# adaLN weights and folded Fourier rows loaded through GpSimd's queue, folds in buffers of their own, three maps in slots

## The chip, the cores and the metric

One core of a Trainium2 chip runs the whole program. The metric is the device time of one execution in microseconds (us); the kernel before takes 1999.18 us, the median of 3 executions (1997.12 to 1999.19). The engines are TensorE (PE), VectorE (DVE), ScalarE (ACT), GpSimd (POOL) and SyncE (SP). A DMA is issued by an instruction on one of these engines, and waits in that engine's instruction order; the profile writes SPq and POOLq for the issuing queue of SP and of POOL.

## The reference, cut to what matters

```python
D_MODEL, SEQ, CTX_LEN, D_FF, N_MOD, DEPTH = 1024, 512, 256, 2816, 9, 2
def modulate(x, shift, scale): return rmsnorm(x) * (1 + scale) + shift
def swiglu(h, w_gu, w_down):
    g, u = jnp.split(h @ w_gu, 2, axis=-1)
    return (jax.nn.silu(g) * u) @ w_down
def fourier_mixer(h, w_out, b_out):
    hg = h.astype(jnp.float32).reshape(Bn, L, C_GROUPS, C_GROUP_CH)
    f = jnp.fft.fftn(hg, axes=(1, 3), norm='ortho').real
    return f.reshape(Bn, L, D_MODEL).astype(h.dtype) @ w_out + b_out
for l in range(DEPTH):                   # layer 0: attention || gMLP, layer 1: Fourier
    m = jnp.split((jax.nn.silu(c) @ ada_w[l] + ada_b[l])[:, None, :], N_MOD, axis=-1)
    x = x + 0.5 * m[2] * swiglu(modulate(x, m[0], m[1]), ffn_w_gu[l, 0], ffn_w_down[l, 0])
    ...                                  # the context tokens the same, in layer 0, with c_ctx
    h = modulate(x, m[3], m[4])
    x = x + m[5] * y                     # y: attention and gMLP, or the Fourier mixer, of h
    x = x + 0.5 * m[8] * swiglu(modulate(x, m[6], m[7]), ffn_w_gu[l, 1], ffn_w_down[l, 1])
return rmsnorm(x, final_norm_g)
```

Everything is float32. The nine modulation vectors `m` of a layer (adaLN: shift, scale and gate of three sub-layers) are a matrix product of one row with a 1024 x 9216 matrix.

## The kernel before, in words

The latent stream stays in SBUF as eight tiles `xs[k]` of 128 channels x 512 tokens. Each product is made of three matmuls (`mm3`, L167 to L171): a weight is split by ACT into a high part `wh` (L162) and by DVE into the rest `wl` (L164), and so is each activation. All weights come through SP's queue: `raw` and `rk` tiles (L161), loaded in the order in which they are used.

**adaLN.** The modulation is not made on PE. The class `Ada` loads 128 rows of the transposed adaLN matrix at a time into a tile `aw` of 128 x 1024 floats (512 KB, `load`, L235), and DVE multiplies it with SiLU(c) on all partitions and sums along the row (`dot`, L240, output `junk`), which gives one column of `modx` (for the context, of `modc`). There are 160 such loads. Those of layer 0 are spread over the first feed-forward network and the attention, with three `aw` buffers; those of layer 1 lie in the last feed-forward network of layer 0 and the first of layer 1, with two buffers (`apool1`, bufs=2).

**A feed-forward network** (`ffn`) goes over 22 slices j of 128 inner channels in chunks of 6, 6, 6 and 4. For each slice PE makes g and u (24 matmuls each), ACT the SiLU, DVE `prod` (L358) = SiLU * u, ACT its high part `ah` (L359), DVE its rest `al` (L360). After a chunk PE multiplies the `ah`, `al` of the chunk with the down weights into `dps`, and DVE adds that to x (L272). A step's extra work is handed to it by hooks: `extra2(j)` puts modulations and folds into step j of the first network of layer 1.

**The folds.** The Fourier mixer's last product uses weights `wf` folded beforehand: `fold(m)` loads 128 rows of wf (`fr`, L1115), DVE adds and subtracts halves (`fold`, L1118 to L1120), ACT and DVE split the result (L1126, L1127), and two stores of 512 KB each put it into `wfd` in DRAM (L1129). Fold 8 holds only a few rows and begins with a memset (L1124). Folds 0 to 8 are made at steps j = 8 to 16 of that network. The `fr` tile is one of the two `aw` buffers of `apool1`.

**The maps.** In the Fourier stage `folded(m)` loads the two parts of map m (`wh` and `wl`, 512 KB each, L1196) from `wfd` into `wpool` tiles, three buffers of each; products `fe` and `fo` use them. `spool` holds equal slots of 128 x 512 floats (`slot`) for activations.

The order of each engine's instructions is set by a scheduler from priorities; `with behind(mark(...))` holds what is in it to the place at which the code calls it.

Of the kernel before, what the change touches and what calls it, by code (L numbers as in the profile page):

```python
# [11 lines left out]
F32 = mybir.dt.float32  # L12
F32R = mybir.dt.float32r
# [6 lines left out]
P = 128  # L20
D = 1024
# [15 lines left out]
DOWN_AT = (0, 0, 0, 0, 0)  # L37

FOLD_AT = 8
IDLE = (5, 8)  # L40
ADA0 = dict(early=4, late=4, first_down=2, down=1, ctx=1)
ADA1 = dict(begin=2, end=20, a=2.2, b=3)
# [6 lines left out]
def kernel(ctx, tc, a):  # L49
    nc = tc.nc  # L50
# [8 lines left out]
    def slot(shape, dtype, name):  # L59
        return spool.tile(shape, dtype, tag="s", name=name)  # L60
# [34 lines left out]
    def nm(s):  # L95
        uid[0] += 1
        return f"{s}_{uid[0]}"

    DVE, ACT, SP = mybir.EngineType.DVE, mybir.EngineType.Activation, mybir.EngineType.SP

    def mark(*engines):

        traced = nc.cur_bb.bb.instructions
        return [next(i for i in reversed(traced) if i.engine == e) for e in engines or (DVE, ACT)]

    @contextmanager
    def behind(last):

        with ExitStack() as st:
            for i in last or ():  # L110
                st.enter_context(tc.issue_after(i))
            yield
# [9 lines left out]
    def banks(name):  # L122

        return pairs.tile([P, 2, 512], F32, tag="pp", name=nm(name))
# [94 lines left out]
    class Ada:  # L219
# [12 lines left out]

        def load(self, l, i):
            w = self.pool.tile([P, D], F32, tag="aw", name=nm("aw"))
            nc.sync.dma_start(w, a["adaT"][l, i])  # L235
            return w

        def dot(self, w, out, c):
# [17 lines left out]
    def col(m, j, k):  # L256
        return m[:, 8 * j + k:8 * j + k + 1]
# [85 lines left out]
    def first_w(l, i):  # L343

        return [kept(a["wgu"][2 * l + i, j, q]) for j in range(2) for q in range(2)]
# [207 lines left out]
    apool = st0.enter_context(tc.tile_pool(name="apool", bufs=3))  # L553
# [98 lines left out]
    def some(us):  # L652
        budget[0] += us
        while jobs and budget[0] >= jobs[0][0]:
            c, f = jobs.pop(0)
            budget[0] -= c
            with behind(mark(DVE, ACT, SP) if len(jobs) < len(rest) or not rest else None):
                f()
# [21 lines left out]
    def mix_w(n):  # L680
        while len(ws) < n:
            ws.append(kept(srcs[len(ws)]))

    mid, _ = ffn(0, 0, h, lambda m: col(modx[0], 2, m), tails, [(0, 8), (8, 5), (13, 5), (18, 4)],
              ctx={"h": hc1, "gate": lambda m: col(modc, 2, m)}, extra=extra0, start=(start_w, start), ahead=lambda: None,
              between=lambda: mix_w(4))
# [63 lines left out]
    def weights(src):  # L750
        w = load_w(src, [P, KD, P])
        return lambda k: (w[0][:, k], w[1][:, k])
# [73 lines left out]
    for t in range(4):  # L826
        for g in range(4):
            i = 4 * t + g
# [24 lines left out]
    for hd in range(1, 4):  # L853
        w = weights(a["wk"][hd])
# [217 lines left out]
    apool = st3.enter_context(tc.tile_pool(name="apool1", bufs=2))  # L1072
# [35 lines left out]
    wfd = [dram.tile([P, 2, D], F32, name=f"wfd{m}") for m in range(KD + 1)]  # L1108

    def fold(m):  # L1110
        raw = apool.tile([P, D], F32, tag="aw", name=nm("fr"))
        sm = raw
        if m < KD:
            sm = apool.tile([P, D], F32, tag="fold", name=nm("fold"), bufs=1)
            nc.sync.dma_start(raw, a["wf"][m].rearrange("p k c -> p (k c)"))  # L1115
            lower, upper = (raw.rearrange("p (k c) -> p k c", k=KD)[:, i::2] for i in range(2))
            both = [sm[:, b:b + 512].rearrange("p (k c) -> p k c", k=4) for b in (0, 512)]
            nc.vector.tensor_tensor(both[0], lower, upper, ALU.add)  # L1118
            nc.vector.tensor_tensor(both[1], upper, lower, ALU.subtract)
            nc.vector.memset(sm[0:1, 512:1024], 0.0)  # L1120
            hi = raw
        else:
            hi = apool.tile([P, D], F32, tag="fold", name=nm("fold"), bufs=1)
            nc.vector.memset(raw, 0.0)  # L1124
            nc.sync.dma_start(raw[0:4].rearrange("g (m c) -> g m c", m=KD), a["wf"][:, 0, 1::2, :].rearrange("m g c -> g m c"))
        nc.scalar.copy(hi.bitcast(F32R), sm)  # L1126
        nc.vector.tensor_tensor(sm.bitcast(F32R), sm, hi, ALU.subtract)  # L1127
        for i, t in enumerate((hi, sm)):
            nc.sync.dma_start(wfd[m][:, i], t)  # L1129

    def extra2(j, m=None):
        if m is None and j < ADA1["end"]:
            some(ADA1["b"])
        if m is None and FOLD_AT <= j <= FOLD_AT + KD:
            fold(j - FOLD_AT)

    mid, w1 = ffn(0, 1, h3, lambda m: col(modx[0], 8, m), tails, chunks, mid=mid, w1=w1,
                  ahead=lambda: first_w(1, 0), extra=extra1)
# [55 lines left out]
    def stored(m, wh, wl):  # L1194
        for i, t in enumerate((wh, wl)):
            nc.sync.dma_start(t.bitcast(F32), wfd[m][:, i])  # L1196

    def folded(m):
        wh = wpool.tile([P, 1024], F32R, tag="wh", name=nm("wh"))
        wl = wpool.tile([P, 1024], F32R, tag="wl", name=nm("wl"))  # L1200
        stored(m, wh, wl)
        return [(wh[:, i * P:i * P + P], wl[:, i * P:i * P + P]) for i in range(8)]
# [8 lines left out]
    for t0, g in [(t0, g) for t0 in (0, 2) for g in range(4)]:  # L1211
        if 2 * t0 + g in (4, 5):
            ps = banks("G")[:, :, :256]
        else:
            ps = bank("G").rearrange("p (t c) -> p t c", t=2)
        for t in range(2):
            ts_ = slice((t0 + t) * P, (t0 + t) * P + P)
            for kt in range(2):
                hk = h5[2 * g + kt]
                cs = slice(256 * kt, 256 * kt + 256)  # L1220
                nc.tensor.matmul(ps[:, t], hk[0][:, ts_], tc_[0][:, cs], start=kt == 0, stop=False)
                nc.tensor.matmul(ps[:, t], hk[0][:, ts_], tc_[1][:, cs], start=False, stop=False)
                nc.tensor.matmul(ps[:, t], hk[1][:, ts_], tc_[0][:, cs], start=False, stop=kt == 1)
        pair = [slot([P, 2, 256], F32R, nm("gt")) for _ in range(2)]
        for t in range(2):
            rt = rtok[:, t0 + t, 0:1]
            nc.scalar.activation(pair[0][:, t], ps[:, t], AF.Copy, scale=rt)
            nc.vector.scalar_tensor_tensor(pair[1][:, t], ps[:, t], rt, pair[0][:, t].bitcast(F32),
                                           ALU.mult, ALU.subtract)
            gh[t0 + t][g] = (pair[0][:, t], pair[1][:, t])  # L1230
        for q in range(2):
            nc.vector.tensor_tensor(nyd[:, t0:t0 + 2, q, g], pair[q][:, :, 128].bitcast(F32), pair[q][:, :, 0].bitcast(F32), ALU.subtract)
        if t0 == 0 and g == 0:
            constant()
            mid[0]()
            mid[1]()
    COS, SIN = slice(0, 258), slice(256, 512)
    ef, of = [], []
    for g in range(4):
# [40 lines left out]
    for m in range(KD):  # L1280
        w = folded(m)
# [22 lines left out]
        if m == 2:  # L1304
            w1 = first_w(1, 1)
    idle(IDLE[0])
    rstd6(SEG[0])
    idle(IDLE[1])
    end6(SEG[0])
# [135 lines left out]
```

## Time and profile before

| what | value |
| --- | --- |
| time, median of 3 (lowest, highest) | 1999.18 us (1997.12, 1999.19) |
| profiled execution's own time | 2007.54 us |
| span of the profiled execution | 2005.8 us |
| mean granted TensorE clock | 0.996 of full speed |
| PE busy | 1968.6 us, 98% |
| DVE busy | 1194.8 us, 60% |
| ACT busy | 706.0 us, 35% |
| POOL busy | 22.3 us, 1% |
| moved by SP's DMA queue (q1) | 288.37 MB, 44.5% of 16 engines' span |
| moved by POOL's DMA queue (q0) | 4.20 MB, 0.8% |

The profile shows one execution, which took 8.4 us longer than the median of the timed ones, and 1.74 us of it lie outside its span. PE is busy nearly throughout, so the places to look at are the few in which it isn't, or in which its matmuls are slow.

### The profile page before, as it was taken

Reading aid. Unit: us, or ns where it says so; the run is one execution under the profiler, and the core shown is the slowest. Engines: PE = TensorE matmul, PEld = TensorE weight load, DVE = VectorE, ACT = ScalarE, POOL = GpSimd, SP = SyncE. Lnnn points to the kernel's source line nnn. Section 1 sums busy time; section 2 is a strip of 40 time slices with the busy share of each in tenths; the row PEclk is TensorE's granted clock in tenths of the full one; section 3 lists DMA queues with packets and bytes.
Section 4 is the critical chain, followed back from the end, with each engine's and each line's share of the span. In section 5 each row is a group of like instructions: output and inputs, shape, how many; then the busy total and the mean of one; then the engine's idle time right before and its main releaser. Section 6 shows DMA issues by size and latency. Waiting matters only on the chain.

```text
span 2005.8 us, 27095 instructions
## 1 busy us (share of the span) xinstructions
PE 1968.6 (98%) x10687; PEld 1704.3 (85%) x10687; DVE 1194.8 (60%) x2160; ACT 706.0 (35%) x1161; POOL 22.3 (1%) x49
## 2 busy tenths in 40 slices
PE   7999999999999999999999999999999999999998
PEld 5878899888998877988888898887878998888887
DVE  7984567466386569845555565566673673334344
ACT  4332224212264257632222343232333642222324
POOL 0000000000000110000000000000000000000000
PEclk9999999999999999999999999999999999999999
DMA  8773346456213632244545533568673142323331
GB/s 293 255 240 116 103 150 223 155 182 215 84 43 111 170 109 64 75 149 135 186 140 178 171 113 107 170 210 274 221 267 121 61 147 83 110 82 108 105 100 43
DMA packets 96742, 294.31 MB, mean 147 GB/s; under 512 B 11717, under 2 KB 15077, under 8 KB 96614
## 3 DMA queue, kind: packets, MB, share of 16 engines
q1 hardware_dynamic: 94950, 288.37, 44.5%
q0 software_dynamic: 1664, 4.20, 0.8%
q8 instruction: 84, 1.38, 0.3%
q14 instruction: 44, 0.36, 0.1%
HBM read 270.50 MB, written 11.53 MB: 141 GB/s over the span
## 4 chain that ended last, share of the span: by engine, by line
PE 85%; DVE 6%; DMA 5%; ACT 2%; issue 1%; SPq 0%; DVEq 0%; ACTq 0%
PE dps L171 9%; PE dps L169 9%; PE dps L170 9%; PE g L169 6%; PE g L170 6%; PE g L171 6%; PE u L169 6%; PE u L170 6%; PE u L171 6%; DMA aw<-in_adaT 3%; PE gc L171 2%; PE gc L170 2%; PE gc L169 2%; DVE junk L240 2%; PE gu L169 1%; PE pj L169 1%
## 5 line engine op out<-in xcount | busy, mean ns | idle before, releaser
L162 ACT CAST wh<-raw 128x1024 fp32r<-128x1024 f32 (+3 forms) x309 | 299.1, 969 | 593.8 <-PE dps L171 257.3
L164 DVE TENSOR_TENSOR wl<-raw,wh 128x1024 fp32r<-128x1024 f32 (+3 forms) x309 | 346.8, 1124 | 258.5 <-ACT wh L162 255.9
L169 PE MATMUL u<-hh,wh 128*128 128x512 f32 (+1 forms) x656 | 249.3, 380 | 0.0
L170 PE MATMUL g<-hh,wl 128*128 128x512 f32 (+1 forms) x656 | 248.9, 379 | 0.0
L169 PE MATMUL g<-hh,wh 128*128 128x512 f32 (+1 forms) x656 | 248.9, 379 | 0.0
L171 PE MATMUL u<-hl,wh 128*128 128x512 f32 (+1 forms) x656 | 248.7, 379 | 0.0
L171 PE MATMUL g<-hl,wh 128*128 128x512 f32 (+1 forms) x656 | 248.7, 379 | 0.0
L170 PE MATMUL u<-hh,wl 128*128 128x512 f32 (+1 forms) x656 | 248.7, 379 | 0.0
L169 PE MATMUL dps<-ah,wh 128*128 128x512 f32 x576 | 226.9, 394 | 6.3 <-ACT ah L359 6.3
L171 PE MATMUL dps<-al,wh 128*128 128x512 f32 x576 | 226.3, 393 | 1.2 <-DVE al L360 1.2
L170 PE MATMUL dps<-ah,wl 128*128 128x512 f32 x576 | 226.3, 393 | 0.0
L272 DVE SCALAR_TENSOR_TENSOR x<-dps,modx,x 128x512 f32<-128x512 f32 (+1 forms) x176 | 106.6, 624 | 142.0 <-PE dps L171 141.6
L240 DVE SCALAR_TENSOR_TENSOR junk<-aw,cb 128x1024 bf16<-128x1024 f32 x144 | 175.4, 1218 | 21.3 <-DMA aw<-in_adaT 21.3
L358 DVE TENSOR_TENSOR prod<-sil,u 128x512 f32<-128x512 f32 (+1 forms) x82 | 54.0, 658 | 180.6 <-PE u L171 178.3
L171 PEld LDWEIGHTS g<-hl,wh 128*128 128x128 f32 x656 | 123.5, 188 | 23.1
L171 PEld LDWEIGHTS u<-hl,wh 128*128 128x128 f32 x656 | 123.5, 188 | 23.0
L169 PEld LDWEIGHTS u<-hh,wh 128*128 128x128 f32 x656 | 123.5, 188 | 23.1
L170 PEld LDWEIGHTS u<-hh,wl 128*128 128x128 f32 x656 | 123.4, 188 | 23.1
L169 PEld LDWEIGHTS g<-hh,wh 128*128 128x128 f32 x656 | 123.5, 188 | 22.8
L170 PEld LDWEIGHTS g<-hh,wl 128*128 128x128 f32 x656 | 123.6, 188 | 22.6
L356 ACT ACTIVATE sil<-g 128x512 f32<-128x512 f32 (+1 forms) x82 | 47.3, 577 | 265.9 <-PE g L171 265.9
L169 PEld LDWEIGHTS dps<-ah,wh 128*128 128x128 f32 x576 | 109.3, 190 | 29.7 <-ACT ah L359 7.5
(355 smaller groups left out, 3693.7 us busy)
## 6 DMA issues: line engine op xcount, KB each, us to landing
raw<-in_wgu SPq DMA_DIRECT2D x172, 512.0 KB, 3.6
aw<-in_adaT SPq DMA_DIRECT2D x160, 512.0 KB, 4.5
raw<-in_wdn SPq DMA_DIRECT2D x72, 384.0 KB, 3.1
raw<-in_wdn SPq DMA_DIRECT2D x16, 512.0 KB, 3.6
rk<-in_wdn SPq DMA_DIRECT2D x32, 256.0 KB, 3.8
rk<-in_wgu SPq DMA_DIRECT2D x24, 256.0 KB, 3.7
raw<-in_wdn SPq DMA_DIRECT2D x16, 320.0 KB, 2.9
wfd<-fr SPq DMA_DIRECT2D x9, 512.0 KB, 2.9
```

The lines of the kernel that those rows point to most:

```text
L162: nc.scalar.copy(wh, raw)
L164: nc.vector.tensor_tensor(wl, raw, wh.bitcast(F32), ALU.subtract)
L169: nc.tensor.matmul(ps, w[0], x[0], start=first, stop=False)
L170: nc.tensor.matmul(ps, w[1], x[0], start=False, stop=False)
L171: nc.tensor.matmul(ps, w[0], x[1], start=False, stop=last)
L240: nc.vector.scalar_tensor_tensor(junk, w, 1.0, c, ALU.mult, ALU.mult, accum_out=out)
L272: nc.vector.scalar_tensor_tensor(xt, ps, gt, xt, ALU.mult, ALU.add)
L356: nc.scalar.activation(s, g, AF.Silu)
L358: nc.vector.tensor_tensor(p, s, u, ALU.mult)
```

## The change: what it does

The loads of `aw`, the loads of `fr` in folds 0 to 7 and all stores to `wfd` are issued by POOL instead of SP (the few rows of fold 8 are still loaded by SP). `fr` gets a buffer of its own instead of one of the two `aw` buffers. `fold` is held to the place at which it is called. Maps 0, 1 and 2 are loaded in quarters of 256 KB (tile `we`, 12 loads by SP) into slots of `spool` and no longer into `wpool` tiles, so that the three buffers there begin with map 3. Line numbers of the changed kernel are larger by 2, after the fold's code by 3 and more.

```diff
+EARLY = (0, 1, 2)
...
         def load(self, l, i):
             w = self.pool.tile([P, D], F32, tag="aw", name=nm("aw"))
-            nc.sync.dma_start(w, a["adaT"][l, i])
+            nc.gpsimd.dma_start(w, a["adaT"][l, i])
             return w
...
     def fold(m):
-        raw = apool.tile([P, D], F32, tag="aw", name=nm("fr"))
+        raw = apool.tile([P, D], F32, tag="fr", name=nm("fr"), bufs=1)
         sm = raw
         if m < KD:
             sm = apool.tile([P, D], F32, tag="fold", name=nm("fold"), bufs=1)
-            nc.sync.dma_start(raw, a["wf"][m].rearrange("p k c -> p (k c)"))
+            nc.gpsimd.dma_start(raw, a["wf"][m].rearrange("p k c -> p (k c)"))
...
         for i, t in enumerate((hi, sm)):
-            nc.sync.dma_start(wfd[m][:, i], t)
+            nc.gpsimd.dma_start(wfd[m][:, i], t)
 
     def extra2(j, m=None):
...
         if m is None and FOLD_AT <= j <= FOLD_AT + KD:
-            fold(j - FOLD_AT)
+            with behind(mark(DVE, ACT, SP)):
+                fold(j - FOLD_AT)
...
+    early = {}
+
+    def folded_early(m):
+
+        w = [[slot([P, 512], F32R, nm("we")) for _ in range(2)] for _ in range(2)]
+        for i in range(2):
+            for b in range(2):
+                nc.sync.dma_start(w[i][b].bitcast(F32), wfd[m][:, i, 512 * b:512 * b + 512])
+        early[m] = [tuple(w[i][q // 4][:, q % 4 * P:q % 4 * P + P] for i in range(2)) for q in range(8)]
+
     def folded(m):
+        if m in early:
+            return early[m]
...
+    for m in EARLY:
+        folded_early(m)
     COS, SIN = slice(0, 258), slice(256, 512)
```

**The start of the program.** SP's rows in the kernel before, from the last two of the eight loads of x on: `vecs` holds biases, `raw` the first weights.

```order
L557 DMA x_100<-in_xT 128x512
L557 DMA x_101<-in_xT 128x512
L558 DMA vecs<-in_vecs 128x161
L235 DMA aw_188<-in_adaT 128x1024
L235 DMA aw_192<-in_adaT 128x1024
L161 DMA raw_203<-in_w 128x1024
L235 DMA aw_231<-in_adaT 128x1024
L235 DMA aw_235<-in_adaT 128x1024
L161 DMA raw_246<-in_w 128x1024
```

In the changed kernel POOL begins as follows (the rows named masks.py make an identity matrix):

```order
masks.py:197 MEMSET ident 128x128
L237 DMA aw_188<-in_adaT 128x1024
masks.py:199 ISA
masks.py:199 AFFINE_SELECT ident<-ident 128x128
L237 DMA aw_192<-in_adaT 128x1024
L237 DMA aw_231<-in_adaT 128x1024
L237 DMA aw_235<-in_adaT 128x1024
```

Before, the first two `aw` stood behind all of x and `vecs`, and two more behind the first `raw`. Now they stand at the head of another queue, and behind `vecs` SP goes on with one `raw` after the other.

**The folds, on the issuing queue.** SP's rows in the kernel before around fold 1's stores (`wfd_8140`) and the load of fold 2 (`fr_12339`):

```order
L235 DMA aw_12324<-in_adaT 128x1024 [waits DMAHW4_49,DMAHW0_49,DVE_49]
L161 DMA raw_12524<-in_wdn 128x768 [waits DVE_49]
L1129 DMA wfd_8140<-fr_12244 128x1024 [waits Activation_49]
L1129 DMA wfd_8140<-fold_12245 128x1024 [waits DMAHW3_49,DVE_49]
L235 DMA aw_12329<-in_adaT 128x1024 [waits DMAHW0_49,DVE_49]
L235 DMA aw_12334<-in_adaT 128x1024 [waits DMAHW5_49,DMAHW2_49]
L161 DMA raw_12550<-in_wdn 128x768 [waits DMAHW6_49,DVE_49]
L1115 DMA fr_12339<-in_wf 128x1024 [waits DMAHW7_49,DMAHW4_49,DVE_49]
```

POOL's rows in the changed kernel around the same stores:

```order
L237 DMA aw_12324<-in_adaT 128x1024 [waits DMASW6_49,DVE_49]
L1117 DMA fr_12244<-in_wf 128x1024 [waits DMASW0_49]
L237 DMA aw_12329<-in_adaT 128x1024 [waits DMASW7_49,DVE_49]
L1131 DMA wfd_8140<-fr_12244 128x1024 [waits Activation_49]
L1131 DMA wfd_8140<-fold_12245 128x1024 [waits DVE_49]
L237 DMA aw_12334<-in_adaT 128x1024 [waits DMASW2_49,DVE_49]
L1117 DMA fr_12339<-in_wf 128x1024 [waits DMASW5_49]
```

`aw_12329` moved ahead of the stores of fold 1; `aw_12334` and the load of fold 2 stand behind them, and the latter waits for the landing of a store (DMASW5).

**The same place on DVE.** The kernel before, from fold 1's last subtraction on:

```order
L1127 TENSOR_TENSOR fold_12245<-fold_12245,fr_12244 128x1024
L240 SCALAR_TENSOR_TENSOR junk_12326,modx_89<-aw_12324,cb_8484 128x1024
L252 SCALAR_TENSOR_TENSOR modx_89<-modx_89,vecs 128x1
L164 TENSOR_TENSOR wl_12470<-raw_12472,wh_12471 128x768
L240 SCALAR_TENSOR_TENSOR junk_12331,modx_89<-aw_12329,cb_8484 128x1024
L358 TENSOR_TENSOR prod_12415<-sil_12413,u_12362 128x512
L252 SCALAR_TENSOR_TENSOR modx_89<-modx_89,vecs 128x1
L240 SCALAR_TENSOR_TENSOR junk_12336,modx_89<-aw_12334,cb_8484 128x1024
L360 TENSOR_TENSOR al_12412<-prod_12415,ah_12411 128x512
```

The changed kernel, from the dot with `aw_12329` on:

```order
L242 SCALAR_TENSOR_TENSOR junk_12331,modx_89<-aw_12329,cb_8484 128x1024
L166 TENSOR_TENSOR wl_12470<-raw_12472,wh_12471 128x768
L254 SCALAR_TENSOR_TENSOR modx_89<-modx_89,vecs 128x1
L242 SCALAR_TENSOR_TENSOR junk_12336,modx_89<-aw_12334,cb_8484 128x1024
L360 TENSOR_TENSOR prod_12415<-sil_12413,u_12362 128x512
L254 SCALAR_TENSOR_TENSOR modx_89<-modx_89,vecs 128x1
L1120 TENSOR_TENSOR fold_12340<-fr_12339 128x512
L1121 TENSOR_TENSOR fold_12340<-fr_12339 128x512
L362 TENSOR_TENSOR al_12412<-prod_12415,ah_12411 128x512
```

The dot with `aw_12329` no longer stands right ahead of `prod_12415`; that with `aw_12334` does, and fold 2's two additions stand between `prod_12415` and `al_12412`.

## Rows read from the trace of the kernel before

**Rows 1.** Waits, all engines: total us, times, longest.

```profile
DVE junk L240 <- DMA aw<-in_adaT: 26.0, 20, 4.8
```

**Rows 2.** A window: length, PE, PEld, DVE, ACT, POOL busy (count), clock, DMA share, GB/s.

```profile
50.00:100.00 50.00, 50.00 (x221) 41.10 (x220) 48.60 (x104) 19.88 (x26) 0.00 (x0) 1.00 0.79 256
```

**Rows 3.** The chain that ended last, single pieces: start, length, what.

```profile
4.40 6.02 DMA x<-in_xT
...
19.21 2.08 PE gu L169 x4
...
110.38 5.33 DMA aw<-in_adaT
...
1606.33 7.03 DMA wl<-wfd
```

**Rows 4.** Timeline of DVE near 116 us: start, length, instruction, [wait].

```profile
115.73 1.23 DVE L240 SCALAR_TENSOR_TENSOR junk<-aw,ccb 128x1024 bf16<-128x1024 f32 x1 [1.49 <-DMA aw<-in_adaT]
```

**Rows 5.** Timeline of PE at the same place.

```profile
118.27 0.50 PE L169 MATMUL dps<-ah,wh 128*128 128x512 f32 x1 [1.62 <-ACT ah L359]
...
119.44 0.50 PE L171 MATMUL dps<-al,wh 128*128 128x512 f32 x1 [0.43 <-DVE al L360]
```

**Rows 6.** Timeline of PE at fold 2.

```profile
1367.65 0.39 PE L171 MATMUL dps<-al,wh 128*128 128x512 f32 x1
1370.81 0.79 PE L169 MATMUL dps<-ah,wh 128*128 128x512 f32 x1 [2.77 <-ACT ah L359]
...
1377.13 0.40 PE L171 MATMUL dps<-al,wh 128*128 128x512 f32 x1
```

**Rows 7.** Timeline of DVE there.

```profile
1368.27 1.22 DVE L240 SCALAR_TENSOR_TENSOR junk<-aw,cb 128x1024 bf16<-128x1024 f32 x1 [4.76 <-DMA aw<-in_adaT]
...
1369.42 0.68 DVE L358 TENSOR_TENSOR prod<-sil,u 128x512 f32<-128x512 f32 x1
...
1371.23 0.68 DVE L360 TENSOR_TENSOR al<-prod,ah 128x512 fp32r<-128x512 f32 x1
```

**Rows 8.** Timeline of SP's queue there.

```profile
1359.94 0.42 SPq L1129 DMA_DIRECT2D wfd<-fr  x1
...
1362.44 2.48 SPq L235 DMA_DIRECT2D aw<-in_adaT  x2
```

**Rows 9.** Timeline of PE at fold 7.

```profile
1471.69 0.39 PE L171 MATMUL dps<-al,wh 128*128 128x512 f32 x1
1473.95 0.50 PE L169 MATMUL dps<-ah,wh 128*128 128x512 f32 x1 [1.87 <-ACT ah L359]
...
1479.48 0.39 PE L169 MATMUL dps<-ah,wh 128*128 128x512 f32 x1
```

**Rows 10.** Timeline of DVE there.

```profile
1470.36 0.69 DVE L1118 TENSOR_TENSOR fold<-fr 128x512 f32<-128x512 f32 x1 [1.02 <-DMA fr<-in_wf]
...
1472.23 0.62 DVE L358 TENSOR_TENSOR prod<-sil,u 128x512 f32<-128x512 f32 x1
```

**Rows 11.** Windows of the start and of four stalls, columns as in rows 2.

```profile
2.00:4.00 2.00, 0.63 (x1) 0.49 (x2) 0.00 (x0) 1.22 (x3) 0.00 (x0) 1.00 0.73 251
...
10.00:12.00 2.00, 2.00 (x2) 0.43 (x2) 1.64 (x6) 1.96 (x4) 0.00 (x0) 1.00 1.02 416
...
115.00:120.00 5.00, 2.95 (x12) 1.82 (x11) 4.26 (x8) 2.38 (x4) 0.00 (x0) 1.00 0.87 301
...
1370.00:1375.00 5.00, 4.19 (x9) 2.95 (x10) 4.55 (x10) 1.45 (x2) 0.00 (x0) 0.51 0.72 207
...
1475.00:1480.00 5.00, 4.50 (x13) 3.57 (x14) 4.58 (x7) 2.40 (x3) 0.00 (x0) 0.66 0.94 298
...
1605.00:1610.00 5.00, 4.46 (x37) 4.28 (x36) 4.19 (x10) 0.73 (x2) 0.00 (x0) 1.00 0.93 330
```

**Rows 12.** The page's DMA issues: count, KB each, median us to landing.

```profile
wfd<-fr SPq DMA_DIRECT2D x9, 512.0 KB, 2.9
```

**Rows 13.** Timeline of POOL's queue, one load of 64 rows.

```profile
746.74 0.52 POOL L871 DMA_DIRECT2D k<-roth  x1
```

## The prediction

> **What bounds the kernel now.** The table of busy times comes first: PE is busy for 98% of the span, so the kernel is bound by PE, and only its few gaps and slow stretches can be won. The second view, the waits, tells which of DVE's waits the moved loads have a part in: DVE waits 20 times for an `aw`, 26.0 us in all [rows 1]. That is no loss by itself, as DVE is idle for 40% of the span. It matters where `prod` or `al`, which PE needs, stand behind such a dot. So the third view is PE's timeline, read for gaps, and beside each the timeline of DVE. At full pace PE starts a matmul each 50.00/221 = 0.226 us [rows 2]. There are four places on which the change bears.
>
> *The start.* The first weight product starts at 19.21; what went before is the landing of the last x, 4.40 + 6.02 = 10.42, and the norm made from it [rows 3].
>
> *116 us.* DVE, busy for 48.60 of the 50 us before [rows 2], waits 1.49 for an `aw` [rows 4] that was issued at 110.38 [rows 3]; `prod` stands right behind that dot, and PE waits 1.62 for `ah` and 0.43 for `al` [rows 5]. With two matmuls slower by 0.11 (0.50 against 0.39) that is about 2.3 us.
>
> *Fold 2.* DVE waits 4.76 for an `aw`, so `prod` starts at 1369.42 and `al` at 1371.23 [rows 7]. PE waits 2.77 and then goes at half speed: 15 matmuls take 1377.13 - 1367.65 = 9.48 us [rows 6] where 15 x 0.226 = 3.39 would do. Lost: 6.1 us. The granted clock of the window is 0.51, near the lower of its two levels (1.2 of 2.4 GHz) [rows 11].
>
> *Fold 7.* DVE waits 1.02 for `fr`, and `prod` stands behind that fold's additions, at 1472.23 [rows 10]. 13 matmuls take 1479.48 - 1471.69 = 7.79 us [rows 9] where 2.94 would do. Lost: 4.85 us, at a clock of 0.66 [rows 11]. The gap of 1.62 at 116 left the clock at 1.00 [rows 11], so what is at stake at the folds is a gap of 2 us plus the slow matmuls behind it.
>
> A small fifth place are the maps: the chain leads through the load of a `wl` issued at 1606.33 [rows 3], and PE is busy for 4.46 of 5 us there [rows 11]. Lost: 0.5.
>
> **The change part by part.** *Loads on POOL at the start: +3.0.* POOL has nothing ahead of its first three `aw` but small memsets, so they run beside the eight x instead of behind them. An `aw` is 0.524 MB, at 416 GB/s 1.26 us [rows 11], three are 3.8. The DMA engines have room for little of that under the x loads: 27% of 2 us, 0.5, in the window 2:4 [rows 11], and I allow 0.2 more behind it. So the last x lands 3.0 us later (bounds: 0, if POOL's issues come late enough to fall behind x, and 3.8). The norm and the first product follow it one for one, since DVE and ACT have nothing to do in between that could be brought forward; the first product is then at 22.2. SP's first `raw` no longer has two `aw` ahead of it, and lands in time.
>
> The Trainium skill (DMA: Bandwidth & Descriptors, "Issuing engines are not separate DMA queues") speaks against a gain here: DMAs of all issuing engines run on the same 16 DMA engines and interleave, so that another queue saves issue time only. This trace agrees where it can be seen, as the engines are near their full share from 4 us on. By the rule alone the sum would hold +3.0 here and nothing for the rest.
>
> *116 us: -1.9.* What DVE has lost there is the sum of small waits for `aw` since the start (those up to 116 us are part of the 26.0 in rows 1). With the loads ahead of x, the first dots find their rows there, and no `raw` holds an `aw` back in SP's order. Against this, POOL takes longer to issue: 64 rows take 0.52 [rows 13], so for 128 rows I estimate twice that, 1.04, where SP takes 0.42 for a store of that size [rows 8]; with three buffers each cycle gets longer by 0.6. DVE's start is 3.0 later, but so is PE's. I take most of the 2.3 as won (bounds: -2.3, and +1.6 if the longer cycle is what counts).
>
> *Fold 2: -5.0.* Now `aw` has both its buffers. The load that stands ahead of `prod` is another one (`aw_12334`); it can go when the dot with `aw_12324` is done, which was at 1362.44 [rows 8] and is about 1 earlier now, as one wait less stands before it (26.0/20 = 1.3 each [rows 1]). A transfer of that size takes 2.9 by SP [rows 12], so about 3.6 by POOL: it lands near 1365.2, the dot (1.22) and `prod` (0.68) end at 1367.1 [rows 7]. PE needs `ah` at 1367.65 + 0.23: just met. But two additions of fold 2 (0.69 each [rows 10]) now stand ahead of `al`, and their `fr` is loaded only when the store of fold 1's high part has landed: 1359.94 [rows 8] + 2.9, then 1.04 for the `aw` issue ahead of it in POOL's order and 3.6 for itself, 1367.5. So `al` is done at 1367.5 + 1.4 + 0.7 = 1369.6, PE needs it at 1367.65 + 3 x 0.226 = 1368.3. A wait of about 1.2 is left, shorter than that at 116 which left the clock alone. Gain 6.1 - 1.1 = 5.0 (bounds 0 and 6.1).
>
> *Fold 7: -4.0.* Its additions now stand ahead of the `al` before, and what stands ahead of `prod` is the memset of fold 8, in the one `fr` buffer, so behind the landing of fold 7's first store. By the same walk the additions come some 4 us earlier than 1470.36, the store lands at 1469.7, the memset (at most the 1.2 of an operation on 1024 columns) ends by 1470.9, `ah` by 1472.3, where PE needs it at 1471.9. Left: 0.4 to 0.8. Gain 4.85 - 0.8 = 4.0 (bounds 0 and 4.85).
>
> *Maps: -0.5.* Twelve loads of 256 KB go out when the slots are free, before the first `fe`, and the three buffers are free for maps 3 to 5 (bounds 0 and -0.5).
>
> *POOL's time* costs nothing elsewhere: some 186 issues of 1.04 are under 200 us of 2000.
>
> Sum: 3.0 - 1.9 - 5.0 - 4.0 - 0.5 = -8.4. Against the profiled execution (2007.54, with 1.74 outside its span of 2005.8) that is 1999.1, with a span of 1997.4. That execution lies 8.4 above the median of the timed ones; I take the difference over as it is, so the forecast for the median is 1999.18 - 8.4 = **1990.8**.
>
> **The rivals.** *(A) POOL's order keeps the stalls.* In POOL's order loads stand behind stores that wait for ACT and DVE, and each must land before a load of the next fold. If the walk is late by 1 to 2 us in one of the two folds, its gap reaches 2 us and the clock falls as before: -8.4 + 4.5 = 1995.3; in both, 1999.8. For it: the margin at fold 2 is nil for `ah`. Against: `aw` gets a second buffer, which is what was missing.
>
> *(B) Slower: a new stall of the same kind.* Nine folds pass through this order. If at one step that ran without a gap before, a load behind a store comes more than 2 us after PE's need, that costs what fold 2 costs now, 6.1, and the same order then keeps the two old stalls as well: 1990.8 + 6.1 + 9.0 = 2005.9, with two new ones 2012. It decides where a store's wait is longer than the lead of the load behind it, some 3 us.
>
> The Trainium skill (SBUF — State Buffer, the box on the "DVE blocks DMA" trap) gives this rival a way: GpSimd writes the descriptors of its own DMAs, and can't while DVE runs an operation in a mode that takes the port pair they share. No run here shows it: the issue in rows 13 took 0.52 with DVE at work beside it.
>
> *(C) The queue was not what held the loads.* The `aw` loads of the first network go out when a buffer comes free; if that alone counts, the -1.9 is nothing: 1992.7. The folds' gain stays, as it comes from the buffer.
>
> **How the numbers follow.** My forecast, with C as a part of it: 0.62, most of it between 1986 and 1995. A: 0.25, 1995 to 2001. B: 0.13, 2001 to 2008. A measurement of this kernel can tell 0.2%, 4 us, from no change, so faster means below 1995.2 and slower above 2003.2: of A a fifth and nearly all the forecast are faster, 0.66; same 0.23; slower 0.11. The range reaches from 1985.2, where all that is lost is won and the start costs nothing (2.3 + 6.1 + 4.85 + 0.5 = 13.8), to 2001.5, into B.
>
> **What would show it.** The first `gu` near 22 instead of 19.2, with x landing around 13.4. No gap of 1.6 near 116. Windows at folds 2 and 7 with a clock of 1.00 and at most 1.2 us of gap. Issues on POOL of about 1 us. No `fe` that waits for a map. The forecast is wrong if POOL's issues are several times longer, if the first product comes no later, or if a window at one of the nine folds has a clock under 0.9.

## The result and the profile after

The changed kernel takes 2019.86 us (median of 4, 2018.06 to 2023.8) against 1998.15 of the kernel before; the ratio is 1.0116, 95% interval 1.0101 to 1.0131. It is slower by 21.7 us where I forecast 8.4 less.

The page of the changed kernel, its head and the two large DMA queues:

```profile
span 2017.5 us, 27187 instructions
...
PE 1970.4 (98%) x10686; PEld 1704.9 (85%) x10687; DVE 1195.2 (59%) x2160; ACT 705.7 (35%) x1161; POOL 121.1 (6%) x235
...
q1 hardware_dynamic: 69030, 190.85, 29.9%
q0 software_dynamic: 28448, 101.73, 15.5%
```

The change did what it says: 97.5 MB more go through POOL's queue (q0), a third of all that is moved. PE's and DVE's busy times are as before, so nothing became more work. What grew is waiting.

The kernel before has to be read from a second profile of it, since the first one lay 8.4 us above the median (first experiment). Windows of that second profile of the kernel before, columns as in rows 2:

```profile
0.00:50.00 50.00, 37.00 (x125) 25.38 (x126) 38.26 (x68) 22.41 (x29) 0.70 (x6) 1.00 0.84 291
100.00:150.00 50.00, 49.57 (x218) 40.58 (x217) 43.49 (x87) 19.38 (x32) 0.00 (x0) 1.00 0.72 238
1350.00:1400.00 50.00, 48.00 (x204) 38.95 (x203) 35.52 (x56) 14.59 (x17) 0.00 (x0) 0.97 0.80 278
1450.00:1500.00 50.00, 49.21 (x217) 40.38 (x216) 36.88 (x62) 19.40 (x26) 1.04 (x3) 1.00 0.79 273
```

The same windows of the changed kernel:

```profile
0.00:50.00 50.00, 33.60 (x101) 22.04 (x102) 34.41 (x62) 20.59 (x27) 8.76 (x21) 0.97 0.78 272
100.00:150.00 50.00, 45.99 (x195) 37.28 (x194) 43.45 (x89) 18.51 (x31) 8.48 (x16) 0.97 0.78 262
1350.00:1400.00 50.00, 46.10 (x191) 37.11 (x190) 36.19 (x62) 14.53 (x18) 10.36 (x20) 0.93 0.74 264
1450.00:1500.00 50.00, 43.25 (x183) 34.90 (x182) 36.47 (x68) 17.93 (x26) 8.54 (x17) 0.93 0.74 251
```

The count behind PE's busy time is the quickest measure of a loss here: at full pace a window of 50 us holds 222 of these matmuls, one per 0.226 us. Before against after: 24, 23, 13 and 34 matmuls fewer, or 5.4, 5.2, 2.9 and 7.7 us. Their sum, 21.2, is the difference of the spans, 2017.5 - 1996.5 = 21.0. So all of it was lost in the windows around the places of the prediction, and in each of them more is lost than before.

PE's timeline of the changed kernel at these places, the rows that answer to [rows 3, 5, 6, 9]:

```profile
22.50 0.80 PE L171 MATMUL gu<-hh,wh 128*128 128x512 f32 x1 [4.57 <-ACT hh L217]
...
123.39 0.50 PE L171 MATMUL dps<-ah,wh 128*128 128x512 f32 x1 [2.44 <-ACT ah L361]
...
1379.61 0.79 PE L171 MATMUL dps<-ah,wh 128*128 128x512 f32 x1 [3.76 <-ACT ah L361]
...
1488.01 0.79 PE L171 MATMUL dps<-ah,wh 128*128 128x512 f32 x1 [5.68 <-ACT ah L361]
```

Behind the wait for `ah` at fold 2, on DVE:

```profile
1364.44 0.69 DVE L1120 TENSOR_TENSOR fold<-fr 128x512 f32<-128x512 f32 x1 [5.03 <-DMA fr<-in_wf]
...
1377.07 1.23 DVE L242 SCALAR_TENSOR_TENSOR junk<-aw,cb 128x1024 bf16<-128x1024 f32 x1 [4.25 <-DMA aw<-in_adaT]
1378.22 0.08 DVE L242 DVE_READ_ACCUMULATOR junk<-aw,cb 128x1 f32 x1
1378.22 0.68 DVE L360 TENSOR_TENSOR prod<-sil,u 128x512 f32<-128x512 f32 x1
```

and on POOL's queue:

```profile
1358.10 0.54 POOL L1117 DMA_DIRECT2D fr<-in_wf  x1 [0.56 <-DMA wfd<-fr]
...
1370.84 0.54 POOL L237 DMA_DIRECT2D aw<-in_adaT  x1 [0.61 <-DVE modx L254]
```

The reader is to see a chain: the `fr` of fold 1 is issued at 1358.10 and lands 6.3 later, DVE waits 5.03 for it and so reads the next `aw` late; that buffer's next load is issued at 1370.84, lands at 1377.05, and `prod` is at 1378.22. The issues take 0.54, half of what I estimated. The landings are what is long here. The DMA issues of that stretch (1349 to 1379) in the changed kernel:

```profile
aw<-in_adaT POOLq DMA_DIRECT2D x6, 512.0 KB, 6.1
raw<-in_wdn SPq DMA_DIRECT2D x4, 384.0 KB, 6.8
wfd<-fr POOLq DMA_DIRECT2D x2, 512.0 KB, 4.1
...
fr<-in_wf POOLq DMA_DIRECT2D x2, 512.0 KB, 6.4
```

and of the same stretch (1342 to 1372) in the second profile of the kernel before, where the median `aw` landed 1.2 sooner and the median `fr` 1.8:

```profile
aw<-in_adaT SPq DMA_DIRECT2D x5, 512.0 KB, 4.9
raw<-in_wdn SPq DMA_DIRECT2D x5, 384.0 KB, 4.9
...
fr<-in_wf SPq DMA_DIRECT2D x2, 512.0 KB, 4.6
```

The largest loss, that at fold 7, has one more link: a dot waits for an `aw`, the additions come late, and `prod` stands behind a memset of the one `fr` buffer, which waits for the store of the fold before. DVE and POOL there:

```profile
1476.04 1.22 DVE L242 SCALAR_TENSOR_TENSOR junk<-aw,cb 128x1024 bf16<-128x1024 f32 x1 [4.14 <-DMA aw<-in_adaT]
...
1478.79 0.68 DVE L1120 TENSOR_TENSOR fold<-fr 128x512 f32<-128x512 f32 x1
...
1482.63 0.54 POOL L1131 DMA_DIRECT2D wfd<-fr  x1 [10.87 <-ACT fr L1128]
...
1485.85 0.91 DVE L1126 MEMSET fr<- 128x1024 f32 x1 [1.31 <-DMA wfd<-fr]
1486.68 0.63 DVE L360 TENSOR_TENSOR prod<-sil,u 128x512 f32<-128x512 f32 x1
```

### The profile page after: what moved, and what is told of

It is laid out like the page before. It is cut to its first block, busy times and chain, and to the rows that moved or that the text cites. A ratio compares the mean times of both kernels' runs of the same rounds, so it can differ in the third digit from the quotient of the medians.

```text
span 2017.5 us, 27187 instructions
## 1 busy us (share of the span) xinstructions
PE 1970.4 (98%) x10686; PEld 1704.9 (85%) x10687; DVE 1195.2 (59%) x2160; ACT 705.7 (35%) x1161; POOL 121.1 (6%) x235
## 4 chain that ended last, share of the span: by engine, by line
PE 87%; DVE 5%; DMA 3%; issue 2%; ACT 2%; POOL 0%; SPq 0%; DVEq 0%; ACTq 0%; POOLq 0%
PE dps L173 9%; PE dps L171 9%; PE dps L172 9%; PE g L171 6%; PE g L172 6%; PE g L173 6%; PE u L171 6%; PE u L173 6%; PE u L172 6%; PE gc L173 2%; PE gc L172 2%; PE gc L171 2%; PE gu L171 2%; PE gu L173 2%; PE gu L172 2%
## 5 line engine op out<-in xcount | busy, mean ns | idle before, releaser
L237 POOL DMA_DIRECT2D aw<-in_adaT x160 | 85.0, 531 | 1067.6 <-DVE modx L254 618.4
```

Source lines behind the costliest of these rows:

```text
L237: nc.gpsimd.dma_start(w, a["adaT"][l, i])
```

## The experiments

PE's matmul counts in the four windows tell for each kernel where it loses; 222 is none, each one less is 0.226 us. (In the first window the start is in the count of every kernel.) Each ratio is against the kernel before, run in the same series; its median there went from 1998.15 to 1999.53.

| kernel | median us | ratio (95%) | 0:50 | 100:150 | 1350:1400 | 1450:1500 |
| --- | --- | --- | --- | --- | --- | --- |
| before, first profile | 1998.15 | 1 | 122 | 211 | 195 | 201 |
| before, second profile | 1998.25 (one run) | | 125 | 218 | 204 | 217 |
| changed | 2019.86 | 1.0116 (1.0101 to 1.0131) | 101 | 195 | 191 | 183 |
| aw_only | 2023.20 | 1.0123 (1.0107 to 1.0139) | 91 | 191 | 175 | 188 |
| folds_only | 2015.70 | 1.0089 (1.0076 to 1.0103) | 119 | 216 | 171 | 187 |
| maps_only | 1997.24 | 0.9994 (0.9985 to 1.0003) | 125 | 214 | 216 | 215 |
| fr_own | 1997.57 | 0.9993 (0.9983 to 1.0003) | 124 | 221 | 222 | 222 |
| fold_queue | 2011.93 | 1.0066 (1.0051 to 1.0081) | 125 | 220 | 184 | 188 |
| aw_start_sp | 2019.13 | 1.0104 (1.0089 to 1.0119) | 120 | 181 | 175 | 186 |
| all_pool | 2019.80 | 1.0105 (1.0090 to 1.0120) | 115 | 192 | 196 | 200 |
| after_sp | 1997.90 | 0.9994 (0.9984 to 1.0004) | 121 | 219 | 212 | 218 |
| aw3_pool | 2013.06 | 1.0073 (1.0057 to 1.0089) | 102 | 187 | 213 | 194 |
| aw_halves | 2005.99 | 1.0041 (1.0026 to 1.0056) | 126 | 199 | 205 | 202 |
| aw3_sp | 1994.89 | 0.9985 (0.9977 to 0.9994) | 125 | 222 | 222 | 217 |
| ring2_sp | 2002.80 | 1.0014 (1.0004 to 1.0025) | 123 | 213 | 212 | 218 |
| raw_pool | 2005.36 | 1.0029 (1.0019 to 1.0039) | 123 | 186 | 213 | 210 |
| aw3_maps | 1994.92 | 0.9977 (0.9968 to 0.9986) | 123 | 214 | 221 | 218 |

A caution holds for all: the scheduler orders DVE's work anew for each kernel, so a dot may stand at another place, and a difference of a few matmuls means little.

**The kernel before once more.** No edit.

> The kernel before, unchanged, profiled a second time, because its first profiled execution took 8.4 us longer than the median of its timed ones, while the changed kernel's took as long as its median. If those 8.4 us are stalls that come and go, this profile has a time near 1998 and smaller losses at 116 us, fold 2 or fold 7 than 2.3, 6.1 and 4.85. If they lie outside these three places, the three losses read the same here and the time differs elsewhere.

It took 1998.25, with a span of 1996.5. The four windows hold 3, 7, 9 and 16 matmuls more than in the first profile, 7.9 us of the 9.3 that the spans differ. So most of the 8.4 were stalls at just the places that I wanted to win.

**The parts, one by one.** First the adaLN loads alone:

```diff
-            nc.sync.dma_start(w, a["adaT"][l, i])
+            nc.gpsimd.dma_start(w, a["adaT"][l, i])
```

> The kernel before with the adaLN loads alone on GpSimd's queue; folds, their buffers and the maps as before. Theory 1 (what the profile after suggests: the loads beside x cost the start, and the first network's dots get their rows later): first product about 3.3 us later, the loss at 116 us up by 3 to 4, folds as before: 1998 + 7 = 2005. Rival (the queue change is neutral apart from the start, and the damage lies in the folds): 2001.

It lost 25, more than the whole change. Against the second profile 34, 27, 29 and 29 matmuls: the start and 120 us as theory 1 had it, but 13.1 us at the folds, which nothing in that theory explains. Then the folds alone (own `fr` buffer, POOL's queue, held to their place; `EARLY = ()`, `aw` on SP):

> The kernel before with the folds' part alone: fr in one buffer of its own, its loads and the stores to wfd on GpSimd's queue, folds held to their place; adaLN loads on SP and maps as before. Theory 1 (the one fr buffer makes a round trip of load, additions, split and store per fold, so DVE waits for fr and all behind it is late): waits for fr of up to 5 us remain, time 1998 + 8 to 14 = 2006 to 2012. Rival (the adaLN loads stuck behind the stores in GpSimd's order are what is late): they aren't behind stores here, so no gap over 1.5 us at the folds, time 1998 or less.

It lost 17.5, 14.2 of it in the two windows of the folds, with 9.04 us from one matmul to the next at fold 2. The rival falls: the adaLN loads stand behind no store here. Theory 1's range (2006 to 2012) was left upward. Last the maps:

```diff
+    for m in EARLY:
+        folded_early(m)
     COS, SIN = slice(0, 258), slice(256, 512)
```

> The kernel before with maps 0 to 2 loaded into slots, nothing else. Theory 1: the wait for a map near 1608 goes, 0.5 us less: 1997.6, which can hardly be told from no change. Rival: the twelve loads hold up SP's queue ahead of the next network's weights and cost more than they give: 2000 or more.

It can't be told from no change; the small wait for a map is gone, and nothing came in its place.

**Buffer or queue?** One edit each:

```diff
# fr_own
-        raw = apool.tile([P, D], F32, tag="aw", name=nm("fr"))
+        raw = apool.tile([P, D], F32, tag="fr", name=nm("fr"), bufs=1)
# fold_queue
-            nc.sync.dma_start(raw, a["wf"][m].rearrange("p k c -> p (k c)"))
+            nc.gpsimd.dma_start(raw, a["wf"][m].rearrange("p k c -> p (k c)"))
-            nc.sync.dma_start(wfd[m][:, i], t)
+            nc.gpsimd.dma_start(wfd[m][:, i], t)
```

> The kernel before with one thing changed: fr in one buffer of its own instead of one of the two that it shared with aw. All loads and stores stay on SP. Theory B (the single buffer: fr of the next fold can be loaded only when a store of the fold before has landed): DVE's waits for fr grow to 5 us, and folds 2 and 7 cost about 7 each more, 1998 + 10 to 15 = 2008 to 2013. Theory Q (two queues: transfers issued side by side on SP and GpSimd share the DMA engines, so the urgent one lands as late as the others): all stands in one queue here, so no loss, 1998 within 4.

> The kernel before with the folds' loads and stores on GpSimd's queue; fr shares the aw buffers as before, and the folds aren't held. Theory Q: the loads of fr and the stores land 1.5 to 2 us later than the 4.5 and 3.2 to 3.7 of before, DVE waits longer, 1998 + 7 to 15. Theory B: the shared buffers are as before, so at most 3 us more.

Theory B, which I had taken from the changed kernel's waits, falls: the single buffer loses nothing, and the queue alone loses 13. A reservation on `fr_own`: the scheduler, free to move the folds, took them out of these windows (DVE is busy for 28.16 us of 1350:1400 against 35.52). `after_sp` below, in which they are held, settles it.

**One queue that is POOL's.** Two kernels:

```diff
# aw_start_sp
+            self.loads += 1
-            nc.sync.dma_start(w, a["adaT"][l, i])
+            (nc.sync if l == 0 and self.loads <= 16 else nc.gpsimd).dma_start(w, a["adaT"][l, i])
# all_pool
-        nc.sync.dma_start(raw, src)
+        nc.gpsimd.dma_start(raw, src)
... (all other loads and stores of SP in the same way, and the holds on SP's place moved to POOL)
```

> The kernel with the adaLN loads alone on GpSimd's queue, but the first 16 of them on SP in their old order. Theory Q: the first product is back at 19.2 and what it cost by 36 us (7.7) is gone; the loss near 120 us (6.3 more than before) stays, as loads of aw and raw still go side by side there, and so do the losses at the folds: 2023 - 7.7 = 2015. Rival (what is lost near 120 us comes from the late start): that goes too, 2023 - 14 = 2009.

> The kernel before with every load and store of SP's queue on GpSimd's queue, in nearly the same order. Theory Q: one queue keeps the order, so urgent loads still go first; an issue takes 0.53 instead of 0.33 us, which is hidden: 1998 to 2004. Rival S (GpSimd's queue as such is slower, its loads land later): the losses near 116 us and at the folds are at least those of the kernel with the adaLN loads alone on GpSimd, 2020 or more.

With the first 16 loads behind x the start is as before (120 against 125 and 91), which shows that part of the mechanism; the loss near 120 stays and is even larger (181), so it doesn't come from the late start. At 2019.13 it is 4 above the 2015 of theory Q. `all_pool` was the surprise: with a single queue in nearly the old order I still lost 21 us, so theory Q alone can't be it. Loads on GpSimd's queue come later there, and the traces show by how much. On SP, in the second profile of the kernel before, a dot's last part and the load that waits for its buffer:

```profile
96.05 0.08 DVE L240 DVE_READ_ACCUMULATOR junk<-aw,ccb 128x1 f32 x1
...
96.16 1.67 SPq L235 DMA_DIRECT2D aw<-in_adaT  x2
```

and on POOL, in `all_pool`:

```profile
98.06 0.08 DVE L240 DVE_READ_ACCUMULATOR junk<-aw,ccb 128x1 f32 x1
...
98.43 0.53 POOL L235 DMA_DIRECT2D aw<-in_adaT  x1 [1.29 <-DVE modc L252]
```

From the dot's end to the issue it is 0.03 us on SP and 0.29 on POOL; over the `aw` loads of each trace that were issued within 0.6 of a dot's end, more than 120 in each, the medians are 0.03 and 0.30. From issue to landing the pages say, first the kernel before:

```profile
raw<-in_wgu SPq DMA_DIRECT2D x172, 512.0 KB, 3.6
aw<-in_adaT SPq DMA_DIRECT2D x160, 512.0 KB, 4.6
```

then `all_pool`:

```profile
raw<-in_wgu POOLq DMA_DIRECT2D x172, 512.0 KB, 3.9
aw<-in_adaT POOLq DMA_DIRECT2D x160, 512.0 KB, 4.8
```

0.2 to 0.3 more. Together each load is about half a microsecond later (theory S). The Trainium skill (DMA: Bandwidth & Descriptors, "Latency and other measured facts") puts the first byte at about 0.6 us for queues like SP's and about 1 for GpSimd's; this difference of 0.4 agrees roughly with the 0.2 to 0.3 at the landing. The 0.27 ahead of the issue is not in it.

**Is half a microsecond enough, and whose is it?** Four kernels:

```diff
# after_sp: the changed kernel, with
-            nc.gpsimd.dma_start(w, a["adaT"][l, i])
+            nc.sync.dma_start(w, a["adaT"][l, i])
... (and the fold's load and stores in the same way)
# aw3_pool (aw on POOL) and aw3_sp (all on SP)
-    apool = st3.enter_context(tc.tile_pool(name="apool1", bufs=2))
+    apool = st3.enter_context(tc.tile_pool(name="apool1", bufs=3))
# aw_halves
-            nc.sync.dma_start(w, a["adaT"][l, i])
+            for s in (slice(0, 512), slice(512, D)):
+                nc.sync.dma_start(w[:, s], a["adaT"][l, i][:, s])
```

> The changed kernel with all its moved loads and stores back on SP; the own buffer of fr, the held folds and the maps in slots stay. Theory S (GpSimd's queue makes each load later: 0.27 us more from a buffer's release to its issue and 0.26 more to its landing, as measured with all loads on it): nothing of the loss is left, 1998 - 2 = 1996 or less. Rival H (holding the folds to their place with one fr buffer costs by itself): 2003 or more.

> The kernel with the adaLN loads alone on GpSimd's queue (2023.2), and three instead of two buffers for layer 1's aw and fr. Theory S with the ring of buffers (a later load only hurts where two buffers leave no lead): of the 13.2 lost at the folds at least 10 go, 2023 - 10 = 2013; the start and the stretch near 120 us stay as they are (14.0 later than before). Rival (a fixed cost of the queue, whatever the lead): 2020 or more.

> The kernel before with each aw load as two loads of 512 columns on SP, which makes the whole land later by one more issue, 0.3 to 0.4 us, with no second queue. Theory S (half a microsecond per load is enough): near 120 us and at the folds together 6 to 12 us lost, 2004 to 2010. Rival (what costs is that two queues share the DMA engines): within 3 of 1998.

> The kernel before with three instead of two buffers for layer 1's aw and fr, all on SP. If the two buffers are what makes the stalls at folds 2 and 7 (Theory S with the ring), the gaps there go: 1998 - 3 to 5 = 1993 to 1995. Rival: the folds' order on DVE makes them, and nothing changes.

`after_sp` differs from the changed kernel in the queue alone, and nothing of the loss is left (1997.90, 0.9994). That is the plainest of the runs: buffer, hold and slots together are neutral, the queue is the 21.7. Its windows at the folds:

```profile
1350.00:1400.00 50.00, 48.64 (x212) 39.29 (x211) 35.18 (x56) 14.57 (x17) 0.00 (x0) 1.00 0.82 293
1450.00:1500.00 50.00, 49.67 (x218) 40.49 (x217) 36.29 (x60) 20.43 (x27) 1.05 (x3) 1.00 0.72 253
```

`aw_halves` has no second queue; it lost 7.5, within the 6 to 12 of theory S, 4.3 near 120 and 3.4 at the last folds. But the delay that its forecast rests on isn't in its trace: from the first half's issue to the second half's landing the median is 4.6, as for a whole `aw` in the kernel before. So it shows that loads issued in another way on SP alone can cost that much, and not the price of half a microsecond. `aw3_pool` gave back 10.1 of what `aw_only` lost, as forecast, most of it at the folds (44 matmuls, 9.9 us): with a third buffer more of the late loads still land in time. `aw3_sp` shows that two buffers made the stall at fold 2 of the kernel before (222 for 204) and takes 1994.89; at fold 7 the second profile had 217 already, and it has 217 too.

**Near 120 us: lead or sharing?**

```diff
# ring2_sp
-    apool = st0.enter_context(tc.tile_pool(name="apool", bufs=3))
+    apool = st0.enter_context(tc.tile_pool(name="apool", bufs=2))
# raw_pool
-        nc.sync.dma_start(raw, src)
+        raws[0] += 1
+        (nc.gpsimd if 8 < raws[0] <= 60 else nc.sync).dma_start(raw, src)
```

> The kernel before, all on SP, with two instead of three aw buffers in layer 0. Theory S with the ring (a buffer's turn is release, issue, landing and dot; the fewer buffers, the less lead a load has): a turn is 5.2 from issue to landing and 1.3 for the dot, so two buffers give a row each 3.2 us where three give one each 2.2; the 41 loads up to 126 us then take 133: PE loses more than 8 us near 120, 2006 to 2025, with no second queue. Rival (the loss near 120 us of the kernels with loads on GpSimd is made by two queues sharing the DMA engines): within 4 of 1998.

> The kernel before with 52 weight loads (raw numbers 9 to 60, the first network's among them) on GpSimd's queue and all aw loads on SP: the two queues are swapped. Theory S (what counts is that the aw loads themselves come half a microsecond later): aw is on the quick queue, raw has lead, so near 120 us at most 2 lost, 1998 to 2001. Theory Q (two queues sharing the DMA engines make the urgent aw land as late as the raw beside it): the sharing is the same, so 4 to 8 lost near 120 us, 2002 to 2007.

`ring2_sp` missed its forecast: 2002.80, below the range, with 1.1 lost near 120 against the second profile (213 for 218) and 4.3 in the window from 50 to 100 (203 matmuls for 222). Fewer buffers cost, but less, and at another place, which speaks against theory S as the whole account. `raw_pool` shows that a second queue costs by itself: all `aw` are on SP, yet 7.2 us are lost near 120. A `raw` issued on POOL at 94.14 and an `aw` issued on SP at 94.83, by that stretch of its DMA issues:

```profile
raw<-in_wdn POOLq DMA_DIRECT2D x1, 512.0 KB, 7.8
aw<-in_adaT SPq DMA_DIRECT2D x1, 512.0 KB, 7.5
```

They landed within 0.4 of one another. In the stretch from 95 to 112 the median `aw` lands 5.8 after its issue and the median `raw` 6.9, where the second profile of the kernel before has 5.1 and 5.0. What the queues moved (packets, MB, share of the 16 engines), first from 95.4 to 97.4, then from 97.4 to 102.2:

```profile
q0 software_dynamic: 95, 0.37, 68.5%
q1 hardware_dynamic: 25, 0.08, 10.8%
...
q1 hardware_dynamic: 371, 1.37, 83.2%
q0 software_dynamic: 52, 0.17, 11.3%
```

So the less urgent `raw` had most of the DMA engines' time just behind the issue of the `aw`. Why the `aw` needed until 102.33 all the same, while SP's queue moved nearly three loads' worth, the trace doesn't show. What waits is an `aw` each time, and behind the second wait `prod`, `ah` and PE:

```profile
102.35 1.23 DVE L242 SCALAR_TENSOR_TENSOR junk<-aw,ccb 128x1024 bf16<-128x1024 f32 x1 [3.54 <-DMA aw<-in_adaT]
...
117.08 1.23 DVE L242 SCALAR_TENSOR_TENSOR junk<-aw,ccb 128x1024 bf16<-128x1024 f32 x1 [1.98 <-DMA aw<-in_adaT]
...
119.57 0.68 DVE L360 TENSOR_TENSOR prod<-sil,u 128x512 f32<-128x512 f32 x1
...
120.95 0.79 PE L171 MATMUL dps<-ah,wh 128*128 128x512 f32 x1 [4.97 <-ACT ah L361]
```

**A version that beats both.** `aw3_sp` with the maps in slots:

> All on SP, three buffers for layer 1's aw and fr, and the maps in slots: the two parts that gave a little by themselves. If the two add, 1998 - 3.6 - 0.9 = 1993.5. Rival: they share what they win, 1994.5 to 1996.

1994.92, 0.9977 (0.9968 to 0.9986), 3 to 6 us less than the kernel before. `aw3_sp` alone has the same median beside another series of the kernel before, so the two can't be told apart here, and what the maps add isn't shown. Its windows at the folds run at or near full pace:

```profile
1350.00:1400.00 50.00, 50.00 (x221) 41.11 (x220) 38.72 (x58) 15.21 (x18) 0.00 (x0) 1.00 0.84 295
1450.00:1500.00 50.00, 49.59 (x218) 40.44 (x217) 30.20 (x50) 17.91 (x24) 1.03 (x3) 1.00 0.69 228
```

## Why the prediction was wrong, point by point

The forecast was 8.4 less, the measurement 21.7 more. By the windows, against the second profile, the terms came out as +5.4 for +3.0 (start), +5.2 for -1.9 (116 us), +2.9 for -5.0 (fold 2) and +7.7 for -4.0 (fold 7). The step that failed is the one behind the last three: that a load on POOL's queue is free of SP's order and so comes sooner, with "about 3.6" for its landing. What the runs showed in its place is that the queue alone makes the loss (`after_sp`): a load on POOL is issued 0.27 later behind the same release, and at the folds (1340 to 1480) the median `aw` of the changed kernel lands 5.9 after its issue and the median `fr` 6.2, against 4.6 and 4.7 before and 4.6 and 4.3 in `all_pool`, which has one queue.

- **The places** were right, all four, and so was what stands behind them: `prod` and `al` behind a dot or an addition that waits for a row.
- **The base** was wrong too: "I take the difference over as it is". The losses of the first profile (2.3 at 116, 6.1 at fold 2, 4.85 at fold 7) are 4, 18 and 5 matmuls in the second, 0.9, 4.1 and 1.1 us: 6.1 to be won, not 13.25. That execution was 8 us above the median mostly because its stalls were larger, and a gain worked out from it came out too large by 7.1. (The range's lower end is 1985.4 by its own sum, 1999.18 - 13.8, and not 1985.2.)
- **The start, +3.0:** right for the first product (22.50 - 19.13 = 3.4). Another 2.0 were lost in the rest of that window: the window's clock is 0.97, and PE goes slower from 33.8 on, behind a dot that waited 1.07 for an `aw`. That `aw` and `raw` side by side made it is not shown.
- **116 us, -1.9:** +5.2. I counted the longer issue (1.04, in truth 0.53) as the queue's whole price, and held that a queue of its own frees `aw` from `raw`. DVE's waits for `aw` between 36 and 126 us are 6.9 us in the changed kernel and 4.1 in the second profile of the kernel before. The median landing there is no longer than before (86 to 122: 4.9 against 5.1), so what is longer for each load is the time up to its issue: 30 loads through three buffers are ten turns, each 0.27 longer, 2.7 us by this estimate.
- **Fold 2, -5.0:** +2.9. "A transfer of that size takes 2.9 by SP, so about 3.6 by POOL" failed. 2.9 was the median landing of a store; with `aw`, `fr` and `raw` in flight at once from two queues the medians are 6.1 to 6.8. The walk was right in its order and 2.5 to 3 us short at each load, where I had found a margin of nil. And the `aw` was not issued earlier than before: in place of "one wait less" DVE waited 5.03 for fold 1's `fr`.
- **Fold 7, -4.0:** +7.7. The same landings made the additions late, but the walk was also wrong in its sum. From the first addition (4 before 1470.36) to the store's issue (1469.7 - 2.9) it leaves 0.4 us; the changed kernel took 3.8 (1478.79 to 1482.63), for the two additions, `al`, a small memset and ACT's part of the split. The first profile already had 3.0 from that addition to the end of the split (1473.37). With that the memset would have held `prod` back for more than 2 us even at the landings that I assumed. The store itself landed in 2.9, as forecast.
- **Maps, -0.5:** the rows named don't show it. PE's one wait in that window of the first profile ended with DVE's `x`, just after a `wh` had landed, and the `wl` issued at 1606.33 landed behind the window, at 1613.36. In the second profile a product does wait for a `wl`, for 0.41, and none does in `maps_only`; the times can't show so little. First the wait of the first profile, then that of the second:

```profile
1609.71 0.36 PE L169 MATMUL fe<-Eh,wh 128*128 128x258 f32 x1 [0.54 <-DVE x L272]
...
1604.51 0.39 PE L170 MATMUL fe<-Eh,wl 128*128 128x258 f32 x1 [0.41 <-DMA wl<-wfd]
```

- **"`aw` gets a second buffer, which is what was missing"** was nearly the right thought: lead was missing. But the own buffer of `fr` gave none to be measured (`after_sp`), a third buffer did (`aw3_sp`).
- **The rivals:** A and B named the place (a load behind stores) but not the cause; `folds_only` has no `aw` behind a store and loses all the same. That DVE holds up POOL's issues, the way given for B, is not seen: from 50 to 100 us of the changed kernel POOL's 12 issues took 6.36 us, 0.53 each, with DVE busy for 49.08. The rule of the Trainium skill that I set beside the first term (DMA: Bandwidth & Descriptors, "Issuing engines are not separate DMA queues") was nearer than my sum, with +3.0: DMAs of all engines run on the same 16 DMA engines. It says that another queue saves issue time only; here a load's issue took 0.53 on POOL against 0.33 on SP.

Three things are shown: the queue makes the whole loss (`after_sp` against the changed kernel); loads on GpSimd's queue cost without a second queue beside it (`all_pool`, 20.9); and a second queue costs though the urgent loads stay on SP (`raw_pool`, 5.8). That the cost in `all_pool` comes from the half microsecond per load is argued and not shown: `aw_halves` doesn't have that delay, and `ring2_sp` missed its forecast. How the two divide the 5.2 near 120 us stays open: either alone gave a loss of that size (5.9 in `all_pool`, 7.2 in `raw_pool`), and a fourth buffer in layer 0, which would tell, wasn't tried.

## What to carry to other kernels

Where loads go out in the order of their urgency and buffers leave no lead, a second queue can cost: in `raw_pool` the less urgent transfer had most of the DMA engines just when the urgent one was issued. Look first for a buffer more, and ask of every load how much later it may land; with each load about half a microsecond later `all_pool` took 20.9 us more. In a walk along a chain, give every operation its own time. Before a gain is worked out from one profiled execution, compare its time with the median, and profile again if it lies above.

## What the runs showed of the hardware

- A load on POOL is issued 0.30 us after the operation that frees its buffer (`all_pool`), one on SP 0.03 (second profile of the kernel before), and a load of 512 KB lands 0.2 to 0.3 later by the medians of the two pages; an issue takes 0.52 to 0.54 us, for 64 rows [rows 13] and for 128 alike.
- A `raw` on POOL and an `aw` on SP, issued 0.69 us apart, landed within 0.4 of one another, after 7.8 and 7.5 us, where the medians of that stretch with SP alone are 5.0 and 5.1. The Trainium skill (DMA: Bandwidth & Descriptors, "Queues, rings and completion order") says that each DMA engine goes round between the queues packet by packet. The trace shows both queues served in turn, but by long stretches (68.5% against 10.8% for 2 us, then 11.3% against 83.2%); what one engine does it doesn't show.
- Behind the gap of 3.16 us at fold 2 of the first profile (1370.81 - 1367.65 [rows 6]) the granted clock was 0.51 [rows 11], and the loss 6.1, about twice the gap; at fold 7 it was a gap of 2.26 (1473.95 - 1471.69 [rows 9]), a clock of 0.66 and a loss of 4.85. The wait of 1.62 at 116 us left the clock at 1.00.
